# Gate and output projections token-major, and long and short matmuls in runs, in a decoder block with three token mixers

## The chip, the cores and the metric

The kernel runs on one core of a Trainium2 chip. The metric is the device time of one execution in microseconds (us), as the median of several. One execution of the kernel before was also recorded by the hardware profiler; all times of single instructions come from that record.

## What is computed

A decoder block on 256 tokens with 2048 features, in float32. Every product with a weight matrix counts here; the mixers themselves stay as they are.

```python
h = rms_norm(x, norm_mix_pre[l])
proj = h @ w_in[l]
a_in, b_in, q, kv, nsa_g, merge_g = jnp.split(proj, splits, axis=-1)
y_a = conformer_conv(a_in, ..., w_a_out[l])            # ends with @ w_a_out
y_b = chunked_spatial_gating(b_in, ..., w_b_out[l])    # ends with @ w_b_out
y_c = native_sparse_attention(q, kv, nsa_g, ..., w_c_out[l])   # ends with @ w_c_out
g_a, g_b, g_c = jnp.split(jax.nn.sigmoid(merge_g), 3, axis=-1)
mixed = (g_a * y_a + g_b * y_b + g_c * y_c) @ w_o[l]
x = x + rms_norm(mixed, norm_mix_post[l])
h = rms_norm(x, norm_ffn_pre[l])
u = causal_depthwise_conv(h @ w_up[l], ffn_conv_w[l], ffn_conv_b[l])
u_g, u_v = jnp.split(u, 2, axis=-1)
x = x + rms_norm((jax.nn.silu(u_g) * u_v) @ w_down[l], norm_ffn_post[l])
```

The merge gates have 3 x 2048 columns; the three output projections go from 1024 features to 2048 each; FFN-up has 11264 columns, FFN-down 5632 rows.

## The kernel before

Each float32 operand of a large product is split into two parts of a shorter float type, a high part and a low one (the rest). A product is then three partial products: high x high, high x low and low x high. Weights come in pieces of 128 x 1024 numbers, 512 KB (`piece`, line 75): SyncE issues the load, ScalarE makes the high part (line 92), VectorE the low part (line 93). Activations are split once, after they are made.

There are two ways to lay a product out.

- Feature-major (`ftile`, line 99, and `mm_f`, line 108): 128 output features are the partitions of the result, the 256 tokens its columns. The weights are the stationary operand, the activations the moving one. For each of the input slices k of 128 features, `mm_f` issues a long matmul of 512 columns (high weights against high and low activations side by side) and a short one of 256 columns (low weights against high activations, added to the second half of the accumulator). The order is long, short, long, short; only in the last slice is the short one first. `fsum` (line 140) then adds the two halves: a ScalarE copy of one, a VectorE add of the other.
- Token-major (`mm_t`, line 120): 128 tokens are the partitions, 512 output features the columns. The activations are stationary, the weights moving, and three long matmuls of 512 columns do one slice for 128 tokens, six for all 256.

The stages, in order: the first normalisation, with transposes; branch A's inputs (16 feature-major tiles, tile name `ps`); branch B's v half (token-major, `pv`) and u half (8 feature-major tiles); columns for the compressed keys and for keys (8 tiles), values (token-major, `pvs`) and queries (8 tiles). Then `branch` (line 658) runs three times, for B, A and C: for every pair of output tiles it makes two gate tiles (`wf_g`, 16 slices each), takes tanh, then makes the two projection tiles (`py`, 8 slices each), scales by the gate and adds to the running sum `mac` (lines 678 to 681). In the third run, `fin` (line 690) splits each finished tile of `mac` into `mh` and `ml`. Next is the output product with `w_o` (`token_major`, line 706, accumulators `po`), a second normalisation with transposes (line 218), FFN-up (88 feature-major tiles from `h2T`, line 785) and FFN-down (`token_major` again).

The mixers run beside this as background work: generators in a queue `bg`, of which `pump` (line 63) takes a share, by estimated cost, after each tile; `until` (line 125) takes as much as is needed before a result is used. The order of instructions on each engine is settled when the program is built, by priority and estimated readiness; each engine's queue runs in order. There are eight banks for accumulators, four for the large products (`acc`) and four for the background (`bg`).

```python
for k in range(KT):
    hi, lo = hs[k // 8]
    mm_f(ps, hi, lo, (k % 8) * 128, mov, k, k == 0, k == KT - 1)
```

Of the kernel before, what the change touches and what calls it, by code (L numbers as in the profile page):

```python
# [19 lines left out]
F32 = mybir.dt.float32  # L20
R = mybir.dt.float32r
AF = mybir.ActivationFunctionType
ALU = mybir.AluOpType
# [3 lines left out]
D = 2048  # L27
T = 256
KT = 16
# [16 lines left out]

@with_exitstack
def block(ctx: ExitStack, tc: tile.TileContext, x, fp, cst, rows, sgw, w1, w2, wf_a, wt_bv, wf_bu, wf_c,
          wt_vs, wf_q, wf_g, wo3, wt_o, wf_up, wt_dn, out):
    nc = tc.nc  # L50
    V, S, PE, G = nc.vector, nc.scalar, nc.tensor, nc.gpsimd

    PZ = ctx.enter_context(tc.tile_pool(name="pz", bufs=1))
    P0 = ctx.enter_context(tc.tile_pool(name="p0", bufs=1))
    PS = ctx.enter_context(tc.tile_pool(name="ps", bufs=4, space=PSUM))
# [4 lines left out]
    bg = deque()  # L60
    debt = [0.0]

    def pump(ns):
        debt[0] = min(debt[0], 0.0) + ns if not bg else debt[0] + ns
        while bg and debt[0] > 0:
            try:
                debt[0] -= next(bg[0])
            except StopIteration:
                bg.popleft()
# [26 lines left out]
    def granule(src):  # L96
        return [piece(src[:, a:a + 1024], 1024) for a in (0, 1024)]

    def ftile(src, mov):

        hs = granule(src)
        ps = PS.tile([128, 2, T], F32, tag="acc", name=f"ps{uid[0]}")
        for k in range(KT):
            hi, lo = hs[k // 8]
            mm_f(ps, hi, lo, (k % 8) * 128, mov, k, k == 0, k == KT - 1)
        return ps

    def mm_f(ps, hi, lo, c, mov, k, first, last):
        def h():
            PE.matmul(ps, lhsT=hi[:, c:c + 128], rhs=mov[:, k], start=first, stop=last)  # L110

        def l():
            PE.matmul(ps[:, 1], lhsT=lo[:, c:c + 128], rhs=mov[:, k, 0], start=False, stop=False,  # L113
                      skip_group_check=True)
        if last:
            l(), h()
        else:
            h(), l()

    def mm_t(ps, xh, xl, hi, lo, first, last):  # L120
        PE.matmul(ps, lhsT=xh, rhs=hi, start=first, stop=False)  # L121
# [3 lines left out]
    def until(name):  # L125

        while name not in marks:
            try:
                debt[0] -= next(bg[0])
            except StopIteration:  # L130
                bg.popleft()
# [8 lines left out]
    def fsum(ps, dst, scale=1.0):  # L140

        t1 = T1["pool"].tile([128, T], F32, tag="q", bufs=T1["bufs"], name=f"t1_{uid[0]}")
        with tc.high_priority(offset=int(PR)):
            S.activation(t1, ps[:, 1], AF.Copy, scale=scale)  # L144
            if scale == 1.0:
                V.tensor_add(dst, ps[:, 0], t1)  # L146
            else:
                V.scalar_tensor_tensor(dst, ps[:, 0], scale, t1, op0=ALU.mult, op1=ALU.add)
# [28 lines left out]
    def q1(name, shape=(128, T)):  # L177
        return P1.tile(list(shape), F32, tag="q", bufs=12, name=name)

    def s16(pool, shape, dt, name):  # L180
        return pool.tile(shape, dt, tag="s16", bufs=1 if pool is P0 else 3, name=name)
# [13 lines left out]
    ident = idn  # L195
# [39 lines left out]
    hT = P0.tile([128, KT, 2, T], R, tag="hT", name="hT")  # L235
# [18 lines left out]
    At = s16(P1, [128, 8, 2, T], R, "At")  # L254
# [55 lines left out]
    BUDGET = BA  # L310
    for j in range(8):
# [9 lines left out]
        pg = ftile(wf_a[2 * j + 1], hT)  # L321
        tg = q1(f"tg{j}")
# [10 lines left out]
    BUDGET = BB  # L333
# [8 lines left out]
    for cb in range(2):  # L342
        pv = [PS.tile([128, 512], F32, tag="acc", name=f"pv{cb}_{t}") for t in range(2)]
        for q in range(4):
            hs = granule(wt_bv[cb * 4 + q])
            for k in range(4 * q, 4 * q + 4):
                hi, lo = hs[(k % 4) // 2]
                c = slice((k % 2) * 512, (k % 2) * 512 + 512)
                for t in range(2):
                    ts = slice(t * 128, t * 128 + 128)  # L350
# [7 lines left out]
    Bt_box = {}  # L358
# [54 lines left out]
    BUDGET = BC  # L413
# [102 lines left out]
    for k in range(KT):  # L516
        hi, lo = piece(wt_vs[:, k * 560:k * 560 + 560], 560)
        for t in range(2):
            ts = slice(t * 128, t * 128 + 128)
# [17 lines left out]
    Ct_box = {}  # L537
# [114 lines left out]


    BUDGET = BG
    mac = s16(P0, [128, KT, T], F32, "mac")
    mh = ml = None

    def branch(bi, act_of, fin):
        for d2 in range(8):
            tgs = []  # L660
            for d in (2 * d2, 2 * d2 + 1):
                pg = ftile(wf_g[bi * 16 + d], hT)
                tg = q1(f"mg{bi}{d}")
                fsum(pg, tg)
                S.activation(tg, tg, AF.Tanh, scale=0.5)
                tgs.append(tg)
                pump(BUDGET)
            hs = granule(wo3[bi * 8 + d2])
            until("BAC"[bi])
            act = act_of()  # L670
            for i, d in enumerate((2 * d2, 2 * d2 + 1)):
                py = PS.tile([128, 2, T], F32, tag="acc", name=f"py{bi}{d}")
                for k in range(8):
                    mm_f(py, hs[i][0], hs[i][1], k * 128, act, k, k == 0, k == 7)
                y = q1(f"y{bi}{d}")
                fsum(py, y)
                if bi == 0:
                    V.scalar_tensor_tensor(mac[:, d], tgs[i], 1.0, y, op0=ALU.add, op1=ALU.mult)
                else:
                    V.scalar_tensor_tensor(y, tgs[i], 1.0, y, op0=ALU.add, op1=ALU.mult)  # L680
                    V.tensor_add(mac[:, d], mac[:, d], y)
                if fin:
                    fin(d)
            pump(BUDGET)

    branch(0, lambda: Bt_box["t"], None)
    branch(1, lambda: At, None)
    until("A")

    def fin(d):  # L690
        S.activation(mh[:, d], mac[:, d], AF.Copy, scale=0.5)
        V.scalar_tensor_tensor(ml[:, d], mac[:, d], 0.5, mh[:, d].bitcast(F32), op0=ALU.mult, op1=ALU.subtract)

    mh = s16(P1, [128, KT, T], R, "mh")
    ml = s16(P1, [128, KT, T], R, "ml")
    branch(2, lambda: Ct_box["t"], fin)


    x2 = s16(P1, [128, 2, D], F32, "x2")
# [6 lines left out]
    def token_major(src, lh, ll, nq, keep, done):  # L706


        nk = 4 * nq
        for cb in range(4):  # L710
            po = [PS.tile([128, 512], F32, tag="acc", name=f"po{nq}{cb}_{t}") for t in range(2)]
            k1 = nk - (keep if cb == 3 else 0)

            def mm(k, t, hi, lo):
                ts = slice(t * 128, t * 128 + 128)
                mm_t(po[t], lh(k)[:, ts], ll(k)[:, ts], hi, lo, k == 0, k == nk - 1)
            for k2 in range(0, k1, 2):
                q = cb * nq + k2 // 4
                hi, lo = piece(src[q][:, (k2 % 4) * 512:(k2 % 4) * 512 + 1024], 1024)
                for i in range(2):  # L720
                    for t in range(2):
                        mm(k2 + i, t, hi[:, i * 512:i * 512 + 512], lo[:, i * 512:i * 512 + 512])
            if cb == 3:
                ws = []
                for k2 in range(k1, nk, 2):
                    q = cb * nq + k2 // 4
                    ws.append(piece(src[q][:, (k2 % 4) * 512:(k2 % 4) * 512 + 1024], 1024, kept))
                for t in range(2):
                    for k in range(k1, nk):
                        hi, lo = ws[(k - k1) // 2]  # L730
                        c = slice((k % 2) * 512, (k % 2) * 512 + 512)
                        mm(k, t, hi[:, c], lo[:, c])
                    done(cb, t, po[t])
            else:
                for t in range(2):
                    done(cb, t, po[t])
# [44 lines left out]
    for i in range(NFT):  # L781
        acc = []
        for v in range(2):
            f = 2 * i + v
# [3 lines left out]
            a = P2.tile([128, T], F32, tag="fa", bufs=4, name=f"fa{f}")  # L788
# [41 lines left out]
def _layout(inp):  # L830
    import numpy as np
    c = np.ascontiguousarray
# [4 lines left out]
    def feat(w, cols):  # L837

        k = w.shape[0] // 128
        w = w[:, cols].reshape(k, 128, -1, 128)  # L840
        return c(w.transpose(2, 1, 0, 3)).reshape(w.shape[2], 128, k * 128)

    def tok(w, cols):

        k = w.shape[0] // 512
        w = w[:, cols].reshape(k, 4, 128, -1, 512)
        return c(w.transpose(3, 0, 2, 1, 4)).reshape(w.shape[3] * k, 128, 2048)
# [15 lines left out]
    up_cols = np.concatenate([np.concatenate([ar(128) + 128 * i, FF + ar(128) + 128 * i]) for i in range(NFT)])  # L863
    c_rows = q_cols - 4096

    def outp(w):
        w = w.reshape(8, 128, 8, 2, 128)
        return c(w.transpose(2, 1, 3, 0, 4)).reshape(8, 128, 2048)

    wo3 = np.concatenate([outp(g["w_b_out"][0]), outp(g["w_a_out"][0]), outp(g["w_c_out"][0][c_rows])])  # L870
    m0 = 6704
    g_cols = np.concatenate([m0 + 2048 + ar(2048), m0 + ar(2048), m0 + 4096 + ar(2048)])

# [29 lines left out]
    for qt in range(2):  # L903
# [9 lines left out]
        "x": c(g["x"].reshape(2, 128, D)), "fp": c(fp), "cst": cst, "rows": c(rows),  # L913
        "sgw": c(g["sg_w"][0].transpose(2, 0, 1)), "w1": w1, "w2": w2,
        "wf_a": feat(w_in, a_cols), "wt_bv": tok(w_in, slice(3072, 4096)), "wf_bu": feat(w_in, slice(2048, 3072)),
        "wf_c": feat(w_in, c_cols), "wt_vs": wt_vs, "wf_q": feat(w_in, q_cols), "wf_g": feat(w_in, g_cols),
        "wo3": wo3, "wt_o": tok(g["w_o"][0], slice(None)), "wf_up": feat(g["w_up"][0], up_cols),
        "wt_dn": tok(g["w_down"][0], slice(None)),
    }

# [17 lines left out]
```

## Time and profile before

| | |
|---|---|
| median of 3 runs | 1648.02 us (1646.96 to 1648.09) |
| profiled execution | 1647.76 us |
| its span, first to last instruction | 1645.5 us |
| TensorE matmuls, busy | 1630.1 us, 8860 instructions |
| TensorE weight loads, busy | 1383.7 us, 8860 instructions |
| VectorE, busy | 1123.5 us, 1847 instructions |
| ScalarE, busy | 878.6 us, 1450 instructions |
| read from memory | 299.13 MB, 183 GB/s over the span |

A row of the profile gives the engine (PE is TensorE's matmuls, PEld its weight loads, DVE VectorE, ACT ScalarE), the line of the program, the operation, and the result and operands by tile name. Matmuls overlap in the pipeline, so the duration of one (0.40 us for a long one) is longer than the distance to the next; what a matmul costs in a stream is read from the starts.

### The profile page before, as it was taken

The numbers are of one execution on the slowest core, as the hardware profiler recorded it, in microseconds if no ns is written. First come the engines' busy times: TensorE is split into PE (matmuls) and PEld (weight loads), VectorE is DVE, ScalarE is ACT, GpSimd is POOL, SyncE is SP. The second block draws the span as 40 slices with busy tenths as digits, with TensorE's granted clock in tenths as the row PEclk, the third lists the DMA queues.
The fourth block names the chain that finished last, engine by engine and source line by source line (L and its number), as shares of the span: only waits on it lengthen the run. The fifth ranks groups of instructions, "written<-read, shape, count | busy, mean of one in ns | idle before, by whom it ended". The sixth has DMA issues, their size and how long they took to land.

```text
span 1645.5 us, 23441 instructions
## 1 busy us (share of the span) xinstructions
PE 1630.1 (99%) x8860; PEld 1383.7 (84%) x8860; DVE 1123.5 (68%) x1847; ACT 878.6 (53%) x1450; POOL 16.1 (1%) x44
## 2 busy tenths in 40 slices
PE   8999999999999999999999999999999999999997
PEld 6888889888887788888887888888888888888886
DVE  5999998876555565666656677777777777544444
ACT  5444545754665664554445655555555555444342
POOL 1000020000000000000000000000000000000000
PEclk9999999999999999999999999999999999999999
DMA  8555556575444355555763555555555555665553
GB/s 289 188 187 192 185 170 209 183 245 181 144 142 140 127 166 168 187 184 191 237 210 105 194 190 183 189 188 183 185 189 189 181 191 184 218 198 193 193 191 116
DMA packets 85440, 303.80 MB, mean 185 GB/s; under 512 B 9808, under 2 KB 10192, under 8 KB 84688
## 3 DMA queue, kind: packets, MB, share of 16 engines
q1 hardware_dynamic: 84096, 298.04, 55.5%
q0 software_dynamic: 944, 4.19, 0.7%
q8 instruction: 69, 1.13, 0.3%
q14 instruction: 43, 0.35, 0.1%
q10 hardware_dynamic: 288, 0.08, 0.0%
HBM read 299.13 MB, written 2.10 MB: 183 GB/s over the span
## 4 chain that ended last, share of the span: by engine, by line
PE 97%; DVE 1%; ACT 1%; DMA 1%; issue 0%; DVEq 0%; SPq 0%; ACTq 0%
PE ps L110 40%; PE ps L113 20%; PE po L121 6%; PE po L123 6%; PE po L122 6%; PE py L110 5%; PE py L113 3%; PE s L598 1%; PE O L630 1%; PE pv L123 1%; PE pv L121 1%; PE pv L122 1%; PE pp L624 1%; PE pvs L121 1%; PE pvs L122 0%; PE pvs L123 0%
## 5 line engine op out<-in xcount | busy, mean ns | idle before, releaser
L93 DVE TENSOR_TENSOR wlo<-wraw,whi 128x1024 fp32r<-128x1024 f32 (+1 forms) x553 | 667.7, 1209 | 295.3 <-ACT whi L92 291.4
L92 ACT ACTIVATE whi<-wraw 128x1024 fp32r<-128x1024 f32 (+1 forms) x553 | 577.5, 1047 | 357.1 <-PE po L123 137.0
L110 PE MATMUL ps<-hT,whi 128*128 128x512 f32 x1408 | 498.8, 399 | 0.9 <-ACT whi L92 0.8
L110 PE MATMUL ps<-h2T,whi 128*128 128x512 f32 x1408 | 490.6, 399 | 0.0
L113 PE MATMUL ps<-hT,wlo 128*128 128x256 f32 x1408 | 383.1, 283 | 0.0
L113 PE MATMUL ps<-h2T,wlo 128*128 128x256 f32 x1408 | 381.0, 281 | 0.0
L110 PEld LDWEIGHTS ps<-hT,whi 128*128 128x128 f32 x1408 | 260.5, 188 | 57.0 <-ACT whi L92 1.2
L110 PEld LDWEIGHTS ps<-h2T,whi 128*128 128x128 f32 x1408 | 258.6, 188 | 56.9
L113 PEld LDWEIGHTS ps<-hT,wlo 128*128 128x128 f32 x1408 | 265.8, 189 | 11.2 <-issue 2.0
L113 PEld LDWEIGHTS ps<-h2T,wlo 128*128 128x128 f32 x1408 | 265.9, 189 | 8.8
L144 ACT ACTIVATE t<-ps 128x256 f32<-128x256 f32 x176 | 67.0, 381 | 250.0 <-PE ps L110 250.0
L121 PE MATMUL po<-whi,gh 128*128 128x512 f32 x336 | 130.7, 389 | 0.0
L123 PE MATMUL po<-whi,gl 128*128 128x512 f32 x336 | 130.7, 389 | 0.0
L122 PE MATMUL po<-wlo,gh 128*128 128x512 f32 x336 | 130.7, 389 | 0.0
L266 DVE SCALAR_TENSOR_TENSOR cv<-hb,fps,cv 128x256 f32<-128x256 f32 x240 | 104.5, 476 | 0.1
L146 DVE TENSOR_TENSOR fs<-ps,t 128x256 f32<-128x256 f32 x88 | 37.3, 424 | 76.0 <-ACT t L144 76.0
L123 PEld LDWEIGHTS po<-whi,gl 128*128 128x128 f32 x336 | 63.1, 188 | 13.2
L122 PEld LDWEIGHTS po<-wlo,gh 128*128 128x128 f32 x336 | 63.1, 188 | 13.1
L121 PEld LDWEIGHTS po<-whi,gh 128*128 128x128 f32 x336 | 63.1, 188 | 13.0
L790 ACT ACTIVATE fa<-fs,fps 128x256 f32<-128x256 f32 x88 | 51.8, 588 | 0.0
L110 PE MATMUL py<-At,whi 128*128 128x512 f32 x128 | 46.1, 401 | 0.0
L110 PE MATMUL py<-Bt,whi 128*128 128x512 f32 x128 | 45.3, 397 | 0.0
(261 smaller groups left out, 1578.7 us busy)
## 6 DMA issues: line engine op xcount, KB each, us to landing
wraw<-in_wf_up_dram SPq DMA_DIRECT2D x176, 512.0 KB, 3.7
wraw<-in_wf_g_dram SPq DMA_DIRECT2D x96, 512.0 KB, 3.7
wraw<-in_wt_dn_dram SPq DMA_DIRECT2D x88, 512.0 KB, 3.8
wraw<-in_wo_dram SPq DMA_DIRECT2D x48, 512.0 KB, 3.9
wraw<-in_wf_a_dram SPq DMA_DIRECT2D x32, 512.0 KB, 4.0
wraw<-in_wt_o_dram SPq DMA_DIRECT2D x32, 512.0 KB, 4.4
wraw<-in_wt_bv_dram SPq DMA_DIRECT2D x16, 512.0 KB, 4.4
wraw<-in_wf_bu_dram SPq DMA_DIRECT2D x16, 512.0 KB, 4.4
```

The costliest lines, as they stand in the source:

```text
L92: S.activation(hi[:, :n], raw[:, :n], AF.Copy)
L93: V.tensor_sub(lo[:, :n], raw[:, :n], hi[:, :n].bitcast(F32))
L110: PE.matmul(ps, lhsT=hi[:, c:c + 128], rhs=mov[:, k], start=first, stop=last)
L113: PE.matmul(ps[:, 1], lhsT=lo[:, c:c + 128], rhs=mov[:, k, 0], start=False, stop=False, skip_group_check=True)
L121: PE.matmul(ps, lhsT=xh, rhs=hi, start=first, stop=False)
L122: PE.matmul(ps, lhsT=xh, rhs=lo, start=False, stop=False)
L123: PE.matmul(ps, lhsT=xl, rhs=hi, start=False, stop=last)
L144: S.activation(t1, ps[:, 1], AF.Copy, scale=scale)
L146: V.tensor_add(dst, ps[:, 0], t1)
L266: V.scalar_tensor_tensor(ca[:, j], hb[:, j, k:k + T], w(j, k), ca[:, j], op0=ALU.mult, op1=ALU.add)
L598: PE.matmul(ps[r][:, jj], lhsT=qf[half[r], gg * 4 + b * hpb + jj, qt * 128:qt * 128 + 128], rhs=kk[half[r], gg, br, 0:nk], start=True, sto ...
L790: S.activation(a, s, AF.Identity, bias=fps[:, C_FB + f:C_FB + f + 1], scale=w[2])
```

## The change

The gate products and the three output projections become token-major, in four blocks of 512 columns. For each block there are two gate accumulators (one for each half of the tokens), tanh straight from them, two projection accumulators, and the product of gate and projection is formed from the accumulators in pieces of 256 columns. The running sum `mac` is token-major, so a new generator `mix_gen` transposes it, four slices of 128 columns for each block in the third branch, and makes `mh` and `ml` from the transposed tiles; it is background work, and `token_major` drains what is left of it. `until` is called before the first projection of a branch. The weight layouts follow.

For the feature-major products that stay, `mm_f` now issues a whole tile: the eight long matmuls of the first half, all sixteen short ones, and the eight long ones of the second half.

```diff
-        for k in range(KT):
-            hi, lo = hs[k // 8]
-            mm_f(ps, hi, lo, (k % 8) * 128, mov, k, k == 0, k == KT - 1)
+        mm_f(ps, hs, mov)
         return ps
 
-    def mm_f(ps, hi, lo, c, mov, k, first, last):
-        def h():
-            PE.matmul(ps, lhsT=hi[:, c:c + 128], rhs=mov[:, k], start=first, stop=last)
-
-        def l():
-            PE.matmul(ps[:, 1], lhsT=lo[:, c:c + 128], rhs=mov[:, k, 0], start=False, stop=False,
+    def mm_f(ps, ws, mov):
+
+
+        def h(k):
+            c = (k % 8) * 128
+            PE.matmul(ps, lhsT=ws[k // 8][0][:, c:c + 128], rhs=mov[:, k], start=(k == 0), stop=(k == n - 1))
+
+        def l(k):
+            c = (k % 8) * 128
+            PE.matmul(ps[:, 1], lhsT=ws[k // 8][1][:, c:c + 128], rhs=mov[:, k, 0], start=False, stop=False,
                       skip_group_check=True)
-        if last:
-            l(), h()
-        else:
-            h(), l()
+        n = 8 * len(ws)
+        m = 8 if n > 8 else 7
+        for k in range(m):
+            h(k)
+        for k in range(n):
+            l(k)
+        for k in range(m, n):
+            h(k)
...
-    mac = s16(P0, [128, KT, T], F32, "mac")
+    mac = s16(P0, [128, 2, D], F32, "mac")
...
-    def branch(bi, act_of, fin):
-        for d2 in range(8):
...
+    def branch(bi, act_of):
+
+        for cb in range(4):
+            pg = [PS.tile([128, 512], F32, tag="acc", name=f"pg{bi}{cb}{t}") for t in range(2)]
+            for q in range(4):
+                hs = granule(wt_g[(bi * 4 + cb) * 4 + q])
+                for k in range(4 * q, 4 * q + 4):
+                    hi, lo = hs[(k % 4) // 2]
+                    c = slice((k % 2) * 512, (k % 2) * 512 + 512)
+                    for t in range(2):
+                        ts = slice(t * 128, t * 128 + 128)
+                        mm_t(pg[t], hT[:, k, 0, ts], hT[:, k, 1, ts], hi[:, c], lo[:, c], k == 0, k == KT - 1)
+                if q < 3:
+                    pump(BUDGET)
+            tgs = {}
+            for t in range(2):
+                for a in range(2):
+                    tgs[t, a] = q1(f"mg{bi}{cb}{t}{a}")
+                    S.activation(tgs[t, a], pg[t][:, a * 256:a * 256 + 256], AF.Tanh, scale=0.5)
             pump(BUDGET)
-
-    branch(0, lambda: Bt_box["t"], None)
-    branch(1, lambda: At, None)
+            py = [PS.tile([128, 512], F32, tag="acc", name=f"py{bi}{cb}{t}") for t in range(2)]
+            for q in range(2):
+                hs = granule(wt_p[(bi * 4 + cb) * 2 + q])
+                if cb == 0 and q == 0:
+                    until("BAC"[bi])
+                act = act_of()
+                for k in range(4 * q, 4 * q + 4):
+                    hi, lo = hs[(k % 4) // 2]
+                    c = slice((k % 2) * 512, (k % 2) * 512 + 512)
+                    for t in range(2):
+                        ts = slice(t * 128, t * 128 + 128)
+                        mm_t(py[t], act[:, k, 0, ts], act[:, k, 1, ts], hi[:, c], lo[:, c], k == 0, k == 7)
+                if q == 0:
+                    pump(BUDGET)
+            for t in range(2):
+                for a in range(2):
+                    cc = slice(cb * 512 + a * 256, cb * 512 + a * 256 + 256)
+                    y = mac[:, t, cc] if bi == 0 else tgs[t, a]
+                    V.scalar_tensor_tensor(y, tgs[t, a], 1.0, py[t][:, a * 256:a * 256 + 256], op0=ALU.add,
+                                           op1=ALU.mult)
+                    if bi:
+                        V.tensor_add(mac[:, t, cc], mac[:, t, cc], y)
+            if bi == 2:
+                bg.append(mix_gen(cb))
+            pump(BUDGET)
+
+    def mix_gen(cb):
+
+        for k in range(4 * cb, 4 * cb + 4):
+            pt = PS.tile([128, T], F32, tag="bg", name=f"pm{k}")
+            for t in range(2):
+                PE.transpose(pt[:, t * 128:t * 128 + 128], mac[:, t, k * 128:k * 128 + 128], ident)
+            S.activation(mh[:, k], pt, AF.Copy, scale=0.5)
+            V.scalar_tensor_tensor(ml[:, k], pt, 0.5, mh[:, k].bitcast(F32), op0=ALU.mult, op1=ALU.subtract)
+            yield 500
+
+    branch(0, lambda: Bt_box["t"])
+    branch(1, lambda: At)
     until("A")
-
-    def fin(d):
-        S.activation(mh[:, d], mac[:, d], AF.Copy, scale=0.5)
-        V.scalar_tensor_tensor(ml[:, d], mac[:, d], 0.5, mh[:, d].bitcast(F32), op0=ALU.mult, op1=ALU.subtract)
...
-    branch(2, lambda: Ct_box["t"], fin)
+    branch(2, lambda: Ct_box["t"])
...
                     for t in range(2):
                         mm(k2 + i, t, hi[:, i * 512:i * 512 + 512], lo[:, i * 512:i * 512 + 512])
+                pump(1e6)
...
```

## Rows read from the trace of the kernel before

**Rows 1.** The page: busy time, granted clock in 40 slices, chain by engine and line.

```profile
PE 1630.1 (99%) x8860; PEld 1383.7 (84%) x8860; DVE 1123.5 (68%) x1847; ACT 878.6 (53%) x1450; POOL 16.1 (1%) x44
...
PEclk9999999999999999999999999999999999999999
...
PE 97%; DVE 1%; ACT 1%; DMA 1%; issue 0%; DVEq 0%; SPq 0%; ACTq 0%
PE ps L110 40%; PE ps L113 20%; PE po L121 6%; PE po L123 6%; PE po L122 6%; PE py L110 5%; PE py L113 3%; PE s L598 1%; PE O L630 1%; PE pv L123 1%; PE pv L121 1%; PE pv L122 1%; PE pp L624 1%; PE pvs L121 1%; PE pvs L122 0%; PE pvs L123 0%
```

**Rows 2.** Waits of PE for data: us in total, times, longest.

```profile
PE pth L218 <- DVE dgh L208: 2.5, 1, 2.5
...
PE ptf L218 <- DVE dgf L208: 1.4, 1, 1.4
PE ps L110 <- ACT whi L92: 0.8, 1, 0.8
```

**Rows 3.** Busy us by stretch: PE, PEld, DVE, ACT, POOL; clock, DMA share.

```profile
50.00:100.00 50.00, 50.00 (x285) 43.41 (x285) 49.39 (x95) 24.44 (x35) 0.00 (x0) 1.00 0.56 184
100.00:150.00 50.00, 50.00 (x239) 41.92 (x238) 49.14 (x89) 24.18 (x29) 0.00 (x0) 1.00 0.58 191
...
329.80:640.00 310.20, 310.20 (x1785) 253.85 (x1784) 188.28 (x408) 186.74 (x414) 1.02 (x4) 1.00 0.50 162
640.00:798.90 158.90, 158.90 (x903) 137.96 (x902) 103.90 (x147) 79.82 (x127) 0.00 (x0) 1.00 0.58 187
...
899.80:1397.20 497.40, 497.40 (x2820) 431.62 (x2819) 360.42 (x530) 287.20 (x442) 0.00 (x0) 1.00 0.57 186
1397.20:1636.30 239.10, 239.10 (x1056) 198.03 (x1055) 113.82 (x107) 96.94 (x106) 0.00 (x0) 1.00 0.58 187
```

**Rows 4.** By tile: duration in ns (min/median/max), first and last start in us, form.

```profile
L110 PE MATMUL ps<-h2T,whi x1408: 390/398/476, 899.8 to 1397.0; 128*128 128x512 f32 x176
...
L121 PE MATMUL po<-whi,gh x336: 388/389/396, 1397.2 to 1635.9; 128*128 128x512 f32 x168
...
L110 PE MATMUL py<-Ct,whi x128: 387/398/404, 674.6 to 798.6; 128*128 128x512 f32 x128
```

**Rows 5.** Timeline of PE, short matmuls in a row: start, duration.

```profile
321.63 0.28 PE L456 MATMUL zp<-whi,bk 128*128 128x256 f32 x1
321.75 0.28 PE L458 MATMUL zp<-wlo,bk 128*128 128x256 f32 x1
321.87 0.28 PE L456 MATMUL zp<-whi,bk 128*128 128x256 f32 x1
...
322.47 0.28 PE L458 MATMUL zp<-wlo,bk 128*128 128x256 f32 x1
```

**Rows 6.** Timeline of PE, a feature-major tile that starts behind background work.

```profile
385.08 0.40 PE L110 MATMUL ps<-hT,whi 128*128 128x512 f32 x1
385.31 0.28 PE L113 MATMUL ps<-hT,wlo 128*128 128x256 f32 x1
385.43 0.39 PE L110 MATMUL ps<-hT,whi 128*128 128x512 f32 x1
...
389.59 0.39 PE L110 MATMUL ps<-hT,whi 128*128 128x512 f32 x1
```

**Rows 7.** Timeline of PE in FFN-up, across a boundary of tiles.

```profile
995.32 0.40 PE L113 MATMUL ps<-h2T,wlo 128*128 128x256 f32 x2
995.56 0.63 PE L110 MATMUL ps<-h2T,whi 128*128 128x512 f32 x2
996.03 0.28 PE L113 MATMUL ps<-h2T,wlo 128*128 128x256 f32 x1
996.15 0.40 PE L110 MATMUL ps<-h2T,whi 128*128 128x512 f32 x1
...
996.50 0.40 PE L110 MATMUL ps<-h2T,whi 128*128 128x512 f32 x1
...
996.86 0.40 PE L110 MATMUL ps<-h2T,whi 128*128 128x512 f32 x1
```

**Rows 8.** Groups of VectorE instructions: busy us, mean ns, idle before.

```profile
L93 DVE TENSOR_TENSOR wlo<-wraw,whi 128x1024 fp32r<-128x1024 f32 (+1 forms) x553 | 667.7, 1209 | 295.3 <-ACT whi L92 291.4
...
L146 DVE TENSOR_TENSOR mg<-ps,t 128x256 f32<-128x256 f32 x48 | 20.1, 419 | 31.6 <-ACT t L144 31.4
L680 DVE SCALAR_TENSOR_TENSOR y<-mg,y 128x256 f32<-128x256 f32 x32 | 13.6, 424 | 1.1
```

**Rows 9.** The chain that ended last, in order of time: start, us.

```profile
894.41 5.62 PE ptf L218 x48
```

More of the change, by code (lines that the diff above doesn't have):

```diff
@@ L48, in block @@
 def block(ctx: ExitStack, tc: tile.TileContext, x, fp, cst, rows, sgw, w1, w2, wf_a, wt_bv, wf_bu, wf_c,
-          wt_vs, wf_q, wf_g, wo3, wt_o, wf_up, wt_dn, out):
+          wt_vs, wf_q, wt_g, wt_p, wt_o, wf_up, wt_dn, out):
     nc = tc.nc
@@ L654, in block @@
     BUDGET = BG
-    mac = s16(P0, [128, KT, T], F32, "mac")
+    mac = s16(P0, [128, 2, D], F32, "mac")
     mh = ml = None
-    def branch(bi, act_of, fin):
-        for d2 in range(8):
[L660 to L683, printed above, removed]
-            pump(BUDGET)
@@ L864, in _layout @@
     c_rows = q_cols - 4096
[L866 to L870, printed above, removed]
+    wt_p = np.concatenate([tok(w, slice(None)) for w in
+                           (g["w_b_out"][0], g["w_a_out"][0], g["w_c_out"][0][c_rows])])
     m0 = 6704
@@ L915, in _layout @@
         "wf_a": feat(w_in, a_cols), "wt_bv": tok(w_in, slice(3072, 4096)), "wf_bu": feat(w_in, slice(2048, 3072)),
-        "wf_c": feat(w_in, c_cols), "wt_vs": wt_vs, "wf_q": feat(w_in, q_cols), "wf_g": feat(w_in, g_cols),
-        "wo3": wo3, "wt_o": tok(g["w_o"][0], slice(None)), "wf_up": feat(g["w_up"][0], up_cols),
+        "wf_c": feat(w_in, c_cols), "wt_vs": wt_vs, "wf_q": feat(w_in, q_cols), "wt_g": tok(w_in, g_cols),
+        "wt_p": wt_p, "wt_o": tok(g["w_o"][0], slice(None)), "wf_up": feat(g["w_up"][0], up_cols),
         "wt_dn": tok(g["w_down"][0], slice(None)),
```

## Prediction

> **What bounds the kernel now.** I read the page's engine totals first: TensorE's matmul row is busy 99% of the span, VectorE 68%, ScalarE 53%, and the granted clock stands at its upper level, 2.4 GHz, in all forty slices [rows 1]. A busy matmul row is modelled, so by itself it proves little. The chain of work that ended last says the same with waits in it: 97% of it is TensorE, most of that the feature-major products at lines 110 and 113 [rows 1]. Then TensorE's waits: two waits for scale factors, one at either normalisation, and one of 0.8 us for a weight piece are the longest that involve data [rows 2]. So nothing feeds TensorE too slowly, and a change pays only if its instruction stream gets shorter. Transfers, VectorE and ScalarE matter only where they stop covering.
>
> The next view is the busy time by stretch, because it gives the cost of one instruction by form. FFN-up (899.8 to 1397.2) is 88 feature-major tiles of 16 pairs, a long matmul (512 columns) and a short one (256): 497.4 us / 1408 = 353.3 ns a pair, 5.653 us a tile. FFN-down (1397.2 to 1636.3) is 1056 token-major long matmuls: 239.1 us / 1055 = 226.6 ns each [rows 3]. The first and last starts of both groups give the same [rows 4].
>
> The timeline explains the pair. 512 columns at 2.4 GHz are 213.3 ns, so a token-major long carries 13.3 ns on top. Eight short ones in a row, from another product of the kernel, start every 0.12 us: seven intervals take 0.84 us, 120 ns each, again 13.3 ns above their 106.7 [rows 5]. A long and a short at these prices make 346.6 ns, and one tile at 385 us does run so: 13 pairs in 4.51 us, 346.9 ns each [rows 6]. The usual pair is 353.3, because every third takes 0.36 us where the others take 0.35 [rows 7]. So the same pairs have a fast and a slow rhythm, and nearly all tiles are in the slow one. I read this as a cost of alternating two lengths, some 6.7 ns a pair, that a run of equal lengths doesn't pay.
>
> **The change, part by part.**
>
> *Gate and output projections.* One step of 128 input features for 512 outputs and 256 tokens is four pairs before (4 x (512 + 256) = 3072 columns) and six long matmuls after (6 x 512 = 3072). Columns are the same; two instructions and the alternation go. Slow rhythm: 4 x 353.3 - 6 x 226.6 = 53.6 ns saved a step; fast rhythm: 4 x 346.9 - 6 x 226.6 = 28.0 ns. There are 3 branches x 4 blocks x (16 + 8) = 288 steps, so 8.1 to 15.4 us. The third branch runs without background work; its projections run from 674.6 to 798.6 us [rows 4]. That is seven and a third rounds of 48 pairs (the last start is 0.24 us short of the end): 124.2 / 352 = 352.9 ns, the slow rhythm, so its 96 steps give 5.1 us. For the other 192 I take 45 ns, nearer the upper end since tiles break into the fast rhythm only behind a piece of background work: 8.6 us. Together 13.7.
>
> The TensorE page of the Trainium skill ("TensorE: Matmul & The Clock Gate", Back-to-back issue gap) puts the gap of isolated matmuls at the columns over 2.4 GHz plus about 2.5 ns. By it a long is 215.8 and a short 109.2 ns, a step would save 4 x 325.0 - 6 x 215.8 = 5 ns, and all 288 steps only 1.5 us. The rows here have 226.6 and 120 for this data type [rows 3, 5], so the trace disagrees.
>
> *Eight long, sixteen short, eight long.* This is on 128 tiles: 88 of FFN-up and 40 earlier (16 of branch A, 8 of u, 8 of compressed and key columns, 8 of queries). Instructions and columns stay; only order changes. At run prices a tile is 16 x (226.6 + 120) = 5.546 us. A boundary between runs isn't free: today's tile ends short, short, long and the next begins long, and from 995.32 to 996.03 these four take 0.71 us instead of 0.693 [rows 7]. I add that 17 ns once a tile: 5.563, a saving of 90 ns. FFN-up: 88 x 90 = 7.9 us. The other 40 could give 3.6; but VectorE is busy 49.39 and 49.14 of 50 us from 50 to 150 us [rows 3], where branch A runs, and may not follow, so I take 3.0 (bounds 1.5 to 3.6).
>
> A run of longs whose moving operand is the activations is not shown by the trace longer than two. Bounds: 226.6 ns from FFN-down (and from the fast tile), and 235 ns from the two longs at the tile boundary (0.47 us from 995.56 to 996.03) [rows 7]. I take the lower: it is what a long costs in the long run in 1056 cases, and the boundary pair follows shorts. Weights need no other pace: the second low half is wanted 2.77 us into a tile, where today it was wanted at 3.06, and a tile's two pieces cost VectorE 2.4 us of 5.6 [rows 8].
>
> *Transposes of the merged activations.* The merge is now token-major, so 32 transposes of 128 columns are added. 48 matmuls of 128 columns before FFN-up took 5.62 us, 117 ns each [rows 9]: 32 x 0.117 = 3.7 us on TensorE, all on the path. Their evictions on ScalarE and VectorE replace those of the old merge, instruction for instruction.
>
> *Evictions.* A block of 512 columns loses eight sums of two halves (a ScalarE copy and a VectorE add each); tanh, scaling and adding stay. That is 96 adds of 0.42 us on VectorE [rows 8]; neither engine bounds this stretch (VectorE 188.3 of 310.2 us, then 103.9 of 158.9 [rows 3]), so it earns nothing. Banks: four accumulators, two for gates and two for projections; gates are read while projections run (8 x 6 x 0.227 = 10.9 us of cover), projections during the next gates. The last four transposed blocks are wanted by the output product after 12 steps, 16.3 us later. None of this should show.
>
> *Waits.* Each of the four groups of transposes follows eight VectorE instructions of 0.42 us [rows 8], 3.4 us. If TensorE's queue, which is in order, holds the transposes too early, the gate matmuls behind them wait, up to 3.4 us each, 13.6 in all; if the next block's matmuls stand before them it is nothing. Background work of the same kind made no wait of TensorE that the list of waits shows [rows 2], so I take 0.5.
>
> *Sum.* -13.7 - 7.9 - 3.0 + 3.7 + 0.5 = -20.4. The profiled execution took 1647.76 us (span 1645.5 and 2.3 around it), 0.3 below the median of the runs, 1648.02. So 1627.4, say 1627 us. Best end: -15.4 - 3.6 - 7.9, without boundary cost (-2.2), + 3.7: 1622.4.
>
> **The rivals.**
>
> *Order pays nothing.* The extra belongs to the activations as moving operand, not to the alternation; runs cost what pairs cost, or 235 and 120 ns, 5.68 us a tile (+3.5 us over 128 tiles). Then only the token-major part is left: -13.7 + 4.2 = -9.5, 1638 to 1642 us. For it: the only long pair in the trace is slow [rows 7]. Against: the fast tile has the same operands [rows 6].
>
> *TensorE waits at the transposes* for the whole VectorE chain, four times: 1627.4 + 13.6 = 1641 us. Against: rows 2.
>
> *The grouped order is slower (the other side).* The rhythm has a slot of 0.36 us in every third pair [rows 7]. If equal neighbours hold the engine in that slot, 16 x 0.361 = 5.776 us a tile, +123 ns on 128 tiles, +15.7 us: -9.5 + 15.7 = +6.2, 1654 us. It decides from the tile at 5.653 + 12.8 / 128 = 5.753 us. Against: the shorts in a row at 120 ns [rows 5].
>
> *Fewer instructions save nothing.* The 13.3 ns above the columns stay with the stretch, not with the instruction; six longs then cost what eight matmuls did. The transposes remain: 1647.8 + 3.7 = about 1651 us, no change by the bound below. Against: the same surplus on 512 and 256 columns [rows 3, 5]. The gap of isolated matmuls from the page of the Trainium skill named above would lead to nearly the same, 1647.8 - 1.5 + 3.7 = 1650 us.
>
> **How the numbers follow.** Forecast 0.67; order pays nothing 0.15; waits at the transposes 0.08; grouped order slower 0.06; fewer instructions save nothing 0.04. The forecast's own range is 1622 to 1634. The range takes in the two faster rivals, 1621 to 1642, and leaves out 0.10 and the tails. A difference of 0.2% (3.3 us) is about what a measurement of this kernel can tell from no change. Faster: 0.67 + 0.15 + 0.08, less a little for tails, 0.88; same 0.06; slower 0.06.
>
> **What would show it.** Right: FFN-up in 489.5 us (5.563 a tile) with longs starting 0.227 and shorts 0.12 us apart; gates and projections at 226.6 ns; 32 transposes in some 3.7 us; no new row among TensorE's waits. Wrong: longs at 0.235 (order pays nothing), a wait of TensorE for the merge or a conversion, or VectorE full in branch A with a wait for its low halves.

## The result and the profile after

| | before | changed |
|---|---|---|
| median | 1647.55 us (1646.96 to 1648.09) | 1625.97 us (1625.49 to 1627.62) |
| span of the profiled execution | 1645.5 us | 1624.1 us |
| ratio | | 0.9871 (95%: 0.9854 to 0.9888) |

The forecast was 1627, with a range of 1621 to 1642. The page of the changed kernel, its engine totals and the chain that ended last:

```profile
PE 1609.6 (99%) x8316; PEld 1359.1 (84%) x8316; DVE 1077.0 (66%) x1751; ACT 858.1 (53%) x1354; POOL 15.7 (1%) x44
...
PE 96%; DVE 2%; ACT 1%; DMA 0%; issue 0%; DVEq 0%; SPq 0%; ACTq 0%
PE ps L111 28%; PE ps L115 15%; PE po L129 7%; PE po L128 7%; PE po L127 6%; PE pg L128 5%; PE pg L129 5%; PE pg L127 5%; PE py L127 3%; PE py L129 3%; PE py L128 3%; PE s L604 1%; PE O L636 1%; PE pv L127 1%; PE pv L129 1%; PE pv L128 1%
```

Beside [rows 1]: TensorE is still busy 99% and still makes nearly the whole chain, so the bound has not moved; its stream is shorter. It issues 544 instructions fewer: the 288 steps lose two each, 576, and the transposes add 32. VectorE and ScalarE lose 96 instructions each, the sums of halves; neither bounds the kernel, so that earns nothing here.

TensorE's waits in the changed kernel (us in total, times, longest), against [rows 2]:

```profile
PE pth L224 <- DVE dgh L214: 2.0, 1, 2.0
PE ptf L224 <- DVE dgf L214: 1.4, 1, 1.4
PE warm L206 <- POOL wz L203: 1.4, 1, 1.4
PE pg L128 <- DVE wlo L93: 0.5, 1, 0.5
PE pth L224 <- DVE hT L228: 0.2, 1, 0.2
```

One wait is new, 0.5 us once, for a low half at the first gate block; the old one of 0.8 us for a high half is gone. TensorE waits for nothing at the transposes.

Where the 21.4 us of span went is read from the busy times by stretch (us; PE, PEld, DVE, ACT, POOL; clock, DMA share, GB/s). First two stretches of the kernel before that its rows above don't have: all from the first tile to the end of the third branch, and from there to FFN-up.

```profile
22.40:798.90 776.50, 775.62 (x4437) 660.38 (x4438) 575.77 (x1082) 430.69 (x787) 10.23 (x26) 1.00 0.55 179
...
798.90:899.80 100.90, 99.49 (x462) 81.46 (x460) 58.38 (x91) 51.06 (x87) 1.08 (x2) 1.00 0.57 188
```

And the changed kernel, the same two and FFN-up and FFN-down:

```profile
21.50:783.90 762.40, 761.86 (x3885) 633.67 (x3886) 531.61 (x980) 405.47 (x690) 10.77 (x28) 1.00 0.58 182
...
783.90:885.80 101.90, 100.47 (x470) 82.28 (x468) 60.12 (x97) 51.55 (x88) 1.08 (x2) 1.00 0.56 186
885.80:1375.80 490.00, 490.00 (x2819) 433.03 (x2819) 356.12 (x530) 291.29 (x442) 0.00 (x0) 1.00 0.61 189
1375.80:1614.90 239.10, 239.10 (x1056) 198.00 (x1055) 113.88 (x107) 97.04 (x106) 0.00 (x0) 1.00 0.61 187
```

From the first tile through the branches 14.1 us went (776.5 to 762.4), in FFN-up 7.4 (497.4 to 490.0, [rows 3]), before the first tile 0.9. The output product and the second normalisation took 1.0 us more: the last eight transposes stand there, among the output product's matmuls. FFN-down, whose instructions did not change, takes 239.1 us in both. The 0.9 us before the first tile is not the change's: that part ends between 20.5 and 23.0 us in the profiled executions of this document, with its longest wait (`pth`, above) between 1.6 and 3.1 us. Without it 20.5 us are left.

The gates and projections run at the price of FFN-down. Two rows of one gate block, 24 long matmuls apart:

```profile
683.11 0.39 PE L127 MATMUL pg<-whi,hT 128*128 128x512 f32 x1
...
688.55 0.39 PE L127 MATMUL pg<-whi,hT 128*128 128x512 f32 x1
```

That is 5.44 us, 226.7 ns each.

The timeline of the changed kernel shows one feature-major tile of FFN-up (start, duration, count of matmuls merged into the row):

```profile
984.27 3.82 PE L111 MATMUL ps<-h2T,whi 128*128 128x512 f32 x16
987.93 2.08 PE L115 MATMUL ps<-h2T,wlo 128*128 128x256 f32 x16
989.84 0.63 PE L111 MATMUL ps<-h2T,whi 128*128 128x512 f32 x2
```

From 984.27 to 989.84 is one period, 5.57 us: sixteen longs (eight of the tile before, eight of this one) from 984.27 to 987.93, 229 ns each, and sixteen shorts to 989.84, 119 ns each. With pairs a tile needed 5.653 (497.4 us / 88, [rows 3]).

### The profile page after: what moved, and what is told of

Its sections match the earlier page's. It is cut to its first block, busy times and chain, and to the rows that moved or that the text cites. A ratio compares the mean times of both kernels' runs of the same rounds, so it can differ in the third digit from the quotient of the medians.

```text
span 1624.1 us, 22138 instructions
## 1 busy us (share of the span) xinstructions
PE 1609.6 (99%) x8316; PEld 1359.1 (84%) x8316; DVE 1077.0 (66%) x1751; ACT 858.1 (53%) x1354; POOL 15.7 (1%) x44
## 4 chain that ended last, share of the span: by engine, by line
PE 96%; DVE 2%; ACT 1%; DMA 0%; issue 0%; DVEq 0%; SPq 0%; ACTq 0%
PE ps L111 28%; PE ps L115 15%; PE po L129 7%; PE po L128 7%; PE po L127 6%; PE pg L128 5%; PE pg L129 5%; PE pg L127 5%; PE py L127 3%; PE py L129 3%; PE py L128 3%; PE s L604 1%; PE O L636 1%; PE pv L127 1%; PE pv L129 1%; PE pv L128 1%
## 5 line engine op out<-in xcount | busy, mean ns | idle before, releaser
L111 PE MATMUL ps<-h2T,whi 128*128 128x512 f32 x1408 | 336.7, 391 | 0.0
L115 PEld LDWEIGHTS ps<-h2T,wlo 128*128 128x128 f32 x1408 | 180.9, 191 | 7.0
L115 PE MATMUL ps<-h2T,wlo 128*128 128x256 f32 x1408 | 183.3, 283 | 0.0
L111 PE MATMUL ps<-hT,whi 128*128 128x512 f32 x640 | 156.7, 392 | 0.1
L128 PE MATMUL pg<-wlo,hT 128*128 128x512 f32 x384 | 150.9, 393 | 0.5 <-DVE wlo L93 0.5
L129 PE MATMUL pg<-whi,hT 128*128 128x512 f32 x384 | 150.8, 393 | 0.0
L127 PE MATMUL pg<-whi,hT 128*128 128x512 f32 x384 | 149.2, 393 | 0.0
L111 PEld LDWEIGHTS ps<-hT,whi 128*128 128x128 f32 x640 | 116.4, 188 | 21.8 <-DVE hT L228 0.3
L115 PEld LDWEIGHTS ps<-hT,wlo 128*128 128x128 f32 x640 | 84.7, 191 | 4.6
L115 PE MATMUL ps<-hT,wlo 128*128 128x256 f32 x640 | 86.6, 283 | 0.0
L129 PEld LDWEIGHTS pg<-whi,hT 128*128 128x128 f32 x384 | 72.1, 188 | 15.4 <-issue 0.7
L127 PEld LDWEIGHTS pg<-whi,hT 128*128 128x128 f32 x384 | 71.9, 188 | 15.5 <-issue 1.0
```

Of the source, the lines that this page charges most:

```text
L111: PE.matmul(ps, lhsT=ws[k // 8][0][:, c:c + 128], rhs=mov[:, k], start=(k == 0), stop=(k == n - 1))
L115: PE.matmul(ps[:, 1], lhsT=ws[k // 8][1][:, c:c + 128], rhs=mov[:, k, 0], start=False, stop=False, skip_group_check=True)
L128: PE.matmul(ps, lhsT=xh, rhs=lo, start=False, stop=False)
L129: PE.matmul(ps, lhsT=xl, rhs=hi, start=False, stop=last)
```

## Experiments

The theory was that of the prediction: a matmul costs its columns plus 13.3 ns as long as its neighbours have its length, and changes of length cost extra. So the token-major part should pay through its own instructions, and the order through FFN-up and the other tiles left. The runs took the two parts apart, varied the number of changes, and then took the change of length away while everything else alternated. The kernel before measured 1647.39 us beside the first four, 1647.1 beside the next three and 1648.33, in one run, beside the last.

**The order alone.** The kernel before with the new order; the projections' eight slices make 7 long, 8 short, 1 long.

```diff
-        for k in range(KT):
-            hi, lo = hs[k // 8]
-            mm_f(ps, hi, lo, (k % 8) * 128, mov, k, k == 0, k == KT - 1)
+        mm_f(ps, hs, mov)
...
-                for k in range(8):
-                    mm_f(py, hs[i][0], hs[i][1], k * 128, act, k, k == 0, k == 7)
+                mm_f(py, [hs[i]], act)
```

> The kernel before with the new order alone: gates and projections stay feature-major, and every feature-major tile issues its long and short matmuls in runs (16 slices: 8 long, 16 short, 8 long; the projections' 8 slices: 7 long, 8 short, 1 long). Theory, alternating lengths costs: FFN-up 490 us as in the changed kernel (5.567 us a tile instead of 5.653), and the 48 gate tiles and 48 projection tiles gain at the same rate, 4 and 1.5 us; with 3.4 on the 40 early tiles the whole is some 16 us below before, 1631 to 1632 us. Rival, the tile's gain in the changed kernel came from elsewhere (fewer VectorE and ScalarE instructions, another schedule): FFN-up stays at 497 us and the time at 1645 to 1648 us.

Measured: 1634.06 us, ratio 0.9919 (0.9904 to 0.9934). Its stretches, from the first tile to the end of the branches and FFN-up:

```profile
23.00:794.40 771.40, 771.19 (x4436) 663.16 (x4437) 573.43 (x1082) 431.91 (x787) 10.10 (x25) 1.00 0.55 179
...
895.40:1385.40 490.00, 490.00 (x2819) 433.03 (x2818) 355.83 (x530) 291.48 (x443) 0.00 (x0) 1.00 0.58 189
```

FFN-up takes 490.0 us with feature-major gates too, and VectorE's and ScalarE's instructions are those of the kernel before, so its gain is the order's alone; the rival that it came from a lighter VectorE or another schedule falls. The whole was 2 to 3 us above what was expected. The place is the stretch before: 776.5 to 771.4 us, 5.1 where 8.9 were expected. The third branch, which has no background work, did gain as expected: its projections start here at

```profile
L111 PE MATMUL py<-Ct,whi x128: 389/389/398, 671.8 to 794.2; 128*128 128x512 f32 x128
```

(that row is by tile: duration in ns, first and last start in us), 122.4 us instead of the 124.0 of [rows 4], 1.6 saved, where the expected rates give 1.7 (some 83 ns on each of 14 gate tiles, 31 on each of 16 projection tiles). So the missing 3 to 4 us belong to the part where background work stands among the tiles. Adding up the times from each matmul's start to the next one's in both traces says where: the feature-major matmuls of the stretch took 639.9 us before and 632.0 here, 7.9 less, but 0.8 of that is the wait for a high half [rows 2], which is gone; the background matmuls among them took 136.5 and 139.4, 3.0 more. So the reordered tiles gained some 7 of the 8.9 us, and the larger part of what is missing is in the background matmuls between them. Some of those tiles' pairs ran in the fast rhythm of [rows 6] before and had little to give; that this is the tiles' share of it, and why the same background matmuls took longer, is not shown.

**The token-major part alone.** The changed kernel with the old pairs and the old swap in the last slice.

```diff
-        m = 8 if n > 8 else 7
-        for k in range(m):
+        for k in range(n - 1):
             h(k)
-        for k in range(n):
             l(k)
-        for k in range(m, n):
-            h(k)
+        l(n - 1)
+        h(n - 1)
```

> The changed kernel with the old order of pairs in the feature-major tiles that remain: the token-major part alone. Theory: FFN-up back to 497.4 us, the gates and projections stretch stays at some 466 us (before 475), the early tiles lose 3 to 4 us; in all 7.4 + 3.5 = 11 us above the changed kernel, 1637 us. Rival, the order matters only together with the token-major part or not at all: FFN-up 490 us and 1626 us.

Measured: 1637.14 us, ratio 0.9937 (0.9922 to 0.9952); 11.2 us above the changed kernel. The same two stretches:

```profile
22.20:787.10 764.90, 764.05 (x3884) 632.83 (x3885) 532.00 (x980) 405.91 (x690) 10.64 (x27) 1.00 0.58 181
...
889.00:1386.50 497.50, 497.50 (x2820) 431.55 (x2819) 360.11 (x530) 287.53 (x443) 0.00 (x0) 1.00 0.61 186
```

FFN-up is back at 497.5 us. The stretch before it is 764.9, 11.6 below the kernel before, and the order then takes 2.5 more from it (762.4). The two parts add up: 13.3 us (order alone) and 10.3 (token-major alone) make 23.6 against 21.4 for both. The difference fits the gate and projection tiles, on which the order can act only as long as they are feature-major: in the stretch with them the order takes 5.1 us from the kernel before, and 2.5 once they are token-major.

**Runs of two.**

```diff
-        m = 8 if n > 8 else 7
-        for k in range(m):
+        for k in range(0, n - 2, 2):
             h(k)
-        for k in range(n):
+            h(k + 1)
             l(k)
-        for k in range(m, n):
-            h(k)
+            l(k + 1)
+        h(n - 2)
+        l(n - 2)
+        l(n - 1)
+        h(n - 1)
```

> The changed kernel with runs of two: two long, two short, and so on (16 changes of length in a tile instead of 31 for pairs and 2 for the long runs). If each change of length costs a fixed time, 107 ns over 31 changes = 3.4 ns each, a tile is 5.546 + 0.055 = 5.60 us and FFN-up 493 us, the whole 1626 + 4 = 1630 us. If the cost is a slot that only a strict long-short rhythm meets, a tile is 5.55 to 5.57 us, FFN-up 488 to 490 us and the whole 1624 to 1626 us. If only long runs help, 5.65 us and 1637 us.

Measured: 1630.98 us, ratio 0.9900 (0.9885 to 0.9915). Its FFN-up by tile:

```profile
L111 PE MATMUL ps<-h2T,whi x1408: 389/396/477, 887.7 to 1380.3; 128*128 128x512 f32 x176
```

First to last long 492.6 us, 5.600 us a tile (with 0.2 us behind the last start). That is the number of the first case, a fixed price for each change (runs of four, below, speak against that case all the same), and half the gain: 53 ns above the 5.547 of 16 longs and 16 shorts at run prices, where pairs are 107 above.

**Pairs without the swap.**

```diff
-        m = 8 if n > 8 else 7
-        for k in range(m):
+        for k in range(n):
             h(k)
-        for k in range(n):
             l(k)
-        for k in range(m, n):
-            h(k)
```

> The changed kernel with pairs, long before short in all 16 slices: the swap in the last slice (short, short, long, long across the tile boundary) is gone, so the alternation never breaks. If alternating itself costs 6.7 ns a pair: 16 x 353.3 = 5.653 us a tile, or 5.64 without the boundary's 17 ns, FFN-up 496 to 497 us, the whole 1636 us. Rival, the swap at the boundary puts every tile into the slow rhythm and an unbroken alternation stays in the fast one (346.7 ns a pair, as one tile of before showed): 5.547 us a tile, FFN-up 488 us, the whole 1624 us, below the changed kernel.

Measured: 1637.2 us, ratio 0.9939 (0.9923 to 0.9956). FFN-up by tile, and its timeline:

```profile
L111 PE MATMUL ps<-h2T,whi x1408: 387/398/478, 887.6 to 1384.8; 128*128 128x512 f32 x176
...
999.71 0.40 PE L111 MATMUL ps<-h2T,whi 128*128 128x512 f32 x1
999.95 0.28 PE L115 MATMUL ps<-h2T,wlo 128*128 128x256 f32 x1
1000.06 0.40 PE L111 MATMUL ps<-h2T,whi 128*128 128x512 f32 x1
...
1000.42 0.40 PE L111 MATMUL ps<-h2T,whi 128*128 128x512 f32 x1
...
1000.77 0.40 PE L111 MATMUL ps<-h2T,whi 128*128 128x512 f32 x1
...
1001.12 0.40 PE L111 MATMUL ps<-h2T,whi 128*128 128x512 f32 x1
...
1001.48 0.40 PE L111 MATMUL ps<-h2T,whi 128*128 128x512 f32 x1
...
1001.83 0.40 PE L111 MATMUL ps<-h2T,whi 128*128 128x512 f32 x1
...
1002.18 0.40 PE L111 MATMUL ps<-h2T,whi 128*128 128x512 f32 x1
...
1002.54 0.40 PE L111 MATMUL ps<-h2T,whi 128*128 128x512 f32 x1
```

First to last long are 1407 pairs in 497.2 us, 353.4 ns each. On the timeline the pairs take 0.35, 0.36, 0.35, 0.35, 0.36, 0.35, 0.35, 0.36 us: the pattern of three of [rows 7], unbroken. So the boundary does not make the slow rhythm; alternation without a break has it too, with the same longer third pair.

**All long.** High and low weights alternate as in the kernel before, and all lengths are equal.

```diff
...
-            PE.matmul(ps[:, 1], lhsT=ws[k // 8][1][:, c:c + 128], rhs=mov[:, k, 0], start=False, stop=False,
+            PE.matmul(ps, lhsT=ws[k // 8][1][:, c:c + 128], rhs=mov[:, k], start=False, stop=False,
                       skip_group_check=True)
...
+        for k in range(n - 1):
             h(k)
...
             l(k)
...
+        l(n - 1)
+        h(n - 1)
```

> The changed kernel with the old alternation of high and low weights in the feature-major tiles, but the low weights' matmul made as long as the other (512 columns, against the high and the low activations, which adds the product low x low). All matmuls of a tile have one length; the weights, the moving operand and the accumulator alternate or repeat as in the kernel before. Theory, the change of length costs: 32 x 226.6 = 7.251 us a tile, every start 0.226 to 0.227 us after the last, the whole 1626 + 128 x 1.684 = 1842 us. Rival, the alternation of high and low weights or of two products costs 6.7 ns a pair: 7.36 us a tile, 1855 us. Rival, activations as moving operand cost 235 ns a long matmul: 7.52 us a tile, 1876 us.

Measured, in one run: 1842.0 us. Its timeline:

```profile
1079.67 0.39 PE L115 MATMUL ps<-h2T,wlo 128*128 128x512 f32 x1
1079.90 0.39 PE L111 MATMUL ps<-h2T,whi 128*128 128x512 f32 x1
...
1081.49 0.39 PE L115 MATMUL ps<-h2T,wlo 128*128 128x512 f32 x1
1081.71 0.39 PE L111 MATMUL ps<-h2T,whi 128*128 128x512 f32 x1
```

From 1079.67 to 1081.49 are eight matmuls, 1.82 us or some 227 ns each, and by tile (first and last start) all of FFN-up is the same:

```profile
L111 PE MATMUL ps<-h2T,whi x1408: 389/389/476, 953.3 to 1591.5; 128*128 128x512 f32 x176
```

2816 longs in 638.2 us, 226.7 ns each, and a whole of 1842 us, the number of the first case. By these 226.7 ns against the 226.6 of FFN-down, activations as the moving operand cost a long matmul nothing extra, and neither does the alternation of weights. This is the bound that the prediction chose without having seen such a run.

**All short.** Each long matmul is cut in two. The accumulator's halves are begun separately here, so the sums are not the reference's; the number, length and order of the matmuls are as told.

```diff
...
+        def part(k, w, o, m, first, last):
+            c = (k % 8) * 128
+            PE.matmul(ps[:, o], lhsT=ws[k // 8][w][:, c:c + 128], rhs=mov[:, k, m], start=first, stop=last,
+                      skip_group_check=True)
...
+            part(k, 0, 0, 0, k == 0, k == n - 1)
+            part(k, 1, 1, 0, k == 0, False)
+            part(k, 0, 1, 1, False, k == n - 1)
```

> The changed kernel with every feature-major long matmul cut into two short ones (256 columns for the high activations, 256 for the low), in the old order by slices: high x high, low x high, high x low, so the halves of the accumulator and the weights alternate and all lengths are equal. Theory, the change of length costs: 48 x 120 = 5.76 us a tile, the whole 1626 + 128 x 0.193 = 1651 us. Rival, the change of accumulator half or of weights costs: 107 ns or more on top, 5.87 us a tile, 1665 us.

Measured, in one run: 1651.66 us. Its FFN-up by tile:

```profile
L111 PE MATMUL ps<-h2T,whi x2816: 277/283/365, 894.1 to 1400.9; 128*128 128x256 f32 x188
```

4224 shorts in 506.8 us, 120.0 ns each. The half of the accumulator and the weights change between two of every three neighbours, and that costs nothing. Of the things that alternate in a pair, both runs leave the change of length to carry the 107 ns.

**The transposes four times.**

```diff
-            for t in range(2):
+            for t in (0, 0, 0, 0, 1, 1, 1, 1):
                 PE.transpose(pt[:, t * 128:t * 128 + 128], mac[:, t, k * 128:k * 128 + 128], ident)
```

> The changed kernel with each of the 32 transposes of the merged activations issued four times into the same place, 96 more. If they lie on the path at some 0.11 us each: 10.2 to 11.2 us more than the changed kernel, 1636 to 1637 us. If TensorE had room for them: 1626 us. If the waits around them are what costs: less than 3 us more.

Measured: 1636.68 us, ratio 0.9938 (0.9922 to 0.9955), 10.7 us above the changed kernel: 112 ns for each of the 96. The first block's group on the timeline:

```profile
689.74 3.65 PE L715 MATMUL pm<-idn,mac 128*128 128x128 f32 x32
693.15 0.48 PE L129 MATMUL pg<-whi,hT 128*128 128x512 f32 x1
```

32 in 3.41 us, 107 ns each. So the added transposes cost their full time: they lie on the path.

**Runs of four.** Is it a fixed price for each change from short to long?

```diff
-        m = 8 if n > 8 else 7
-        for k in range(m):
-            h(k)
-        for k in range(n):
-            l(k)
-        for k in range(m, n):
-            h(k)
+        for g in range(0, n, 4):
+            last = g == n - 4
+            for k in range(g, g + 4 - last):
+                h(k)
+            for k in range(g, g + 4):
+                l(k)
+            if last:
+                h(n - 1)
```

> The changed kernel with runs of four (four changes from short to long in a tile). Over the run prices of 5.546 us the tile costs 107 ns with 16 such changes (pairs), 53 ns with 8 (runs of two) and 20 ns with 1 (the changed kernel). If a change from short to long costs the same 6.6 ns however long the run of shorts: 26 ns, 5.573 us a tile, FFN-up 490.4 us. If the cost of a change grows with the shorts before it, from 6.6 ns after two to 20 ns after sixteen: some 8.5 ns each, 34 ns, 5.580 us a tile, FFN-up 491.0 us.

Measured, in one run: 1631.1 us. Its FFN-up by tile:

```profile
L111 PE MATMUL ps<-h2T,whi x1408: 387/396/475, 887.4 to 1380.3; 128*128 128x512 f32 x176
```

492.9 us, 5.603 us a tile: as slow as runs of two, and neither 5.573 nor 5.580. Over the run prices the four orders cost 107 ns a tile (16 changes from short to long, in pairs without the swap), 53 (8), 57 (4) and 20 (1), that is 6.7, 6.6, 14 and 20 ns a change. So the price of a change is not fixed: it is larger in longer runs. Both expectations were wrong.

The traces tell where the price sits. The sixteen longs of the changed kernel's tile above, on the timeline in two narrow windows:

```profile
984.27 1.32 PE L111 MATMUL ps<-h2T,whi 128*128 128x512 f32 x5
...
985.44 2.65 PE L111 MATMUL ps<-h2T,whi 128*128 128x512 f32 x11
987.93 0.76 PE L115 MATMUL ps<-h2T,wlo 128*128 128x256 f32 x5
```

The first five longs behind the change take 1.17 us up to the next start, the other eleven 2.49 us, 226 ns each. Over all tiles of FFN-up, from start to start, those five are late by 6.7, 9.0, 1.9, 5.8 and 4.1 ns, 27 together; from the sixth on a long takes 226.7. The first two shorts of the next run come 7 ns early, which leaves the 20. Counted the same way, the longs of a run lose 10 ns in pairs, 13 in runs of two and 21 in runs of four, and the shorts give back 3, 6 and 7. So a run of longs goes on losing up to its fifth, and a shorter run only stops earlier. How many shorts stand ahead hardly matters from two on: the first long behind two, four and sixteen of them is 6.4, 7.4 and 6.7 ns late.

## Why the prediction was right

*Bound.* TensorE's stream, with cover everywhere else: the page after and the waits say the same, and the order alone paid with the other engines' instructions unchanged.

*Token-major.* The prediction put 13.7 us on the 288 steps, 3.7 on the transposes and 0.5 on waits, net 9.5. The token-major part alone gave 10.3; with 32 transposes at 112 ns (3.6 us) the steps gave 13.8. The guess of 45 ns a step where background work runs held in the sum; it was not measured by itself.

*Order.* FFN-up: 7.9 predicted, 7.5 measured (497.5 with pairs kept, 490.0 in the changed kernel). The 40 early tiles: 3.0 predicted; from start to start their matmuls took 226.9 us with pairs and 223.5 in the changed kernel, 3.4 less, of which 0.8 is a wait for a high half that the first of the two kernels has and the second has not: 2.6. The gate blocks behind them took 0.8 longer, 0.5 of it in the new wait, so the two waits nearly cancel, and the whole stretch gained 2.5. Together 10.9 predicted, and 10.0 in the two stretches. The medians are 11.2 apart; of the 11.0 between the two spans, 0.7 lie before the first tile and 0.3 behind FFN-down, where the order does nothing. That the medians come so near to 10.9 is in part chance.

*Bounds.* A long run was to cost 226.6 ns rather than 235: the run with all matmuls long decided it. A short run 120 ns: the run with all short.

*Where it was off, though it cost nothing in the sum.* The prediction read 17 ns at two longs behind two shorts and put them on a boundary between runs, once a tile. The boundary is right, the one change from short to long, and a tile loses 20 ns there. But the price is made otherwise: 27 ns in five longs, less 7 ns in the shorts that follow. The slow rhythm was read as a slot in every third pair, and as a cost of alternating lengths; without the swap the slot is there in the same place, so alternation makes it, but what sets its period is not shown. The wait of 0.5 us was expected at the transposes and came at the first gate block; that the size fits is chance.

*The rivals.* Order pays nothing fell with the order alone (FFN-up 490.0 us); waits at the transposes with the list of waits; the slower grouped order with its tile, 5.57 us where it decided from 5.753; fewer instructions save nothing with the token-major part alone: the alternation that goes is worth at most 4 x 6.7 = 27 ns a step, and a step gained 48. The gap of isolated matmuls that the Trainium skill gives ("TensorE: Matmul & The Clock Gate", Back-to-back issue gap: columns over 2.4 GHz plus 2.5 ns) would, as an estimate, have let that part gain 1.5 us before its transposes. That gap is for isolated matmuls, and the streams here do not follow it: 226.7 and 120.0 ns with equal matmuls, 13.3 ns above the columns at either length, and 10.3 us gained with the transposes in.

*Open.* Why the longs behind a short one are late, and why up to the fifth, no run here shows. Nor does any show why some tiles among background work, as the one of [rows 6], alternate lengths at 346.9 ns a pair, with no such cost: a change of length is needed for it, but does not always bring it. None of the other versions measured was faster than the changed kernel. What is left of this cost in it is, as an estimate, 128 tiles x 20 ns = 2.6 us.

## What to carry to other kernels

Where TensorE's queue never waits, count what a matmul costs above its columns from the starts in a stream of equals, and prefer the layout with fewer and longer instructions for the same columns: here some 48 ns for every eight that became six (13.8 us over 288 steps), 36 after paying for the transposes. At the run prices the two instructions fewer are some 27 of the 48 (4 x 346.7 - 6 x 226.7); the rest is alternation that went with them, part of which the new order would have saved too. Where two lengths are needed, issue each in one long run; runs of two or of four gave only half of it. Try the two parts apart before believing either, since they share tiles.

## What the runs showed of the hardware that was not expected

A change from short to long has no fixed price: 6.7 ns in pairs, 6.6 in runs of two, 14 in runs of four, 20 in runs of sixteen. The cost is spread over the first five longs behind the change (27 ns in runs of sixteen), and two shorts behind the next change give 7 ns of it back. Alternating weights, changing halves of an accumulator and the kind of moving operand cost nothing that can be seen, 226.7 and 120.0 ns in streams of 2816 and 4224 matmuls.
